# A decoder trunk reads x transposed first, applies the first norm's scale to v, q and k, and squares the MLP on ScalarE

## The chip, the cores and the metric

The kernel runs on one core of one Trainium2 chip. The metric is the time of one execution on the device in microseconds (us), lower is better. The engines: TensorE (PE in the profile; its weight loads are a row of their own, PEld), VectorE (DVE), ScalarE (ACT), GpSimd (POOL) and SyncE (SP), which issues most of the DMAs.

## The reference

Two decoder layers on 512 tokens of width 1024, all in float32. Layer 0 mixes by an attention with forget gates, layer 1 by a short gated convolution. After the mixer come an MLP with a squared ReLU and a gated per-layer embedding. Each of the three sub-layers has an RMSNorm ahead of it (of the input) or behind it (of the result).

```python
def rmsnorm(x, g):
    return x * rsqrt(mean(x * x, axis=-1) + 1e-6) * g

for i in range(2):
    hn = rmsnorm(x, g[0])
    m = fox_attention(hn, ...) if i == 0 else short_conv(hn, ...)
    x = x + rmsnorm(m, g[1])
    f = square(relu(rmsnorm(x, g[2]) @ w_up)) @ w_down        # 1024 -> 4096 -> 1024
    x = x + rmsnorm(f, g[3])
    gate = sigmoid(rmsnorm(x, g[4]) @ w_ple_gate)
    x = x + rmsnorm((p[i] @ w_ple_proj) * gate, g[5])

def fox_attention(h, w_in, b_f, w_out):                       # 16 heads of 64
    q, k, v, f = split(h @ w_in)
    c = cumsum(log_sigmoid(f + b_f))
    s = (q / 8) @ k.T + c[:, None] - c[None, :]               # causal
    return (softmax(s) @ v) @ w_out
```

The scale that the norm gives a token, r = rsqrt(mean(x * x) + 1e-6), is one number for a row of x; the gain g is one number for a column.

## The kernel before, in words

Every float32 operand of a large product is kept as two tiles, a high part rounded to the format fp32r and a low part that is the remainder. `split` (L231) makes them: ScalarE casts the high part (L233), VectorE or GpSimd subtracts (L234). `mm3` (L223) makes a product of three matmuls: high by high (L225), low stationary by high moving (L226), high stationary by low moving (L227). The names of the operands say which is which: in `v<-wh,hTl` the moving tile stands first (wh, the weight's high part) and the stationary one second (hTl, the activations' low part). Where activations are stationary (v, the mixer's output projection, the MLP's last group, the embedding's gate), the weights move; in the q/k, up and convolution projections the weights are stationary (`narrow`) and the activations move.

Weights come in tiles of 128 x 512 in a fixed order (`plan`, L97). `fetch` (L116) issues their loads on SP into 14 raw buffers, `prepare` (L136) splits them, and `wide` (L161) asks for a tile and prepares some tiles beyond it (`soon`). All other tiles share 70 pages of 128 x 512, and PSUM's eight banks are handed out by `bank`.

**The order of the instructions** on an engine is set by a scheduler with a model of the times, except inside `manual_schedule` blocks, where the engines named keep the order in which the code is written.

**The head.** `load_x` (L318) brings x in blocks of 128 tokens. For each block, `stats` (L259) lets ScalarE sum the squares (L256) and GpSimd make r (L248, L251). `scaled` (L262) multiplies x by r and g on VectorE (L264), where g was spread over the partitions by matmuls of a row with ones (L883). `turned` (L270) transposes the result on TensorE (L273), and `keep` (L276) splits it into hT. All of this for block t+1 lies between the products of block t.

**v.** `values(c, t)` (L403) makes chunk c of v for token block t: 8 products over the depth (k) into one bank. The chunks are 272 wide (the last 256 columns of v and the 16 forget-gate logits), 512 and 256. `keep_v` (L417) adds the forget bias (L419) and splits v in pieces of 64 columns (L429). `logs` (L362) and `sums_of_logs` (L384) turn the logits into running sums, with eight small matmuls (L388), which go out to DRAM and come back to each head as a bias (`bias`, L467).

**q and k.** `project(i)` (L435) makes the keys (s = 1) and queries (s = 0) of heads 2i and 2i+1, each 24 matmuls of 512 columns into one bank, and splits them from PSUM, queries with the factor 1/8 (L454, L455). The projections are woven into the loop over scores (`scores`, L485), transposes of the weights (`turn`, L509) and the mixing of v (`mix`, L523).

**The MLP** (`mlp`, L713) goes in eight groups of 512 hidden columns. `up` (L719) makes 24 matmuls for each 128 columns and applies relu on ScalarE (L731); `square` (L717) squares on VectorE. In the first seven groups the squares are taken apart into sums of quarters for a product with fewer multiplications: `halves` (L734) splits them, `quarters` (L742) makes the sums on GpSimd (L745 to L755), and `down` (L759) makes the products A11, A12, A22, S1 and so on, whose results VectorE adds up (L777). In the last group ScalarE squares straight into the high part (L807), VectorE squares again in full (L809, by L717) and subtracts for the low part, hl (L810); then `dn` uses it with activations stationary.

**The embedding's gate** weights get their gain while they are split: ScalarE multiplies by a column (L152), VectorE multiplies and subtracts in one instruction (L153).

Of the kernel before, what the change touches and what calls it, by code (L numbers as in the profile page):

```python
# [41 lines left out]
LATE = 0  # L42
PLE_OFF = 34000
# [22 lines left out]
def trunk(ctx: ExitStack, tc, g4T, x, pT, g, wv, wqk, bf, wo, wci, cw, wco, wup, wdn, wpp, wpg, out):  # L66
# [156 lines left out]
    def mm3(ps, a, b, start, stop):  # L223

        nc.tensor.matmul(ps, a.hi, b.hi, start=start, stop=False)  # L225
        nc.tensor.matmul(ps, a.lo, b.hi, start=False, stop=False)  # L226
        nc.tensor.matmul(ps, a.hi, b.lo, start=False, stop=stop)  # L227
        streamed[0] += 3 * ps.shape[-1]
        due()

    def split(hi, lo, src, eng=nc.vector):  # L231

        nc.scalar.copy(hi, src)  # L233
        eng.tensor_tensor(out=lo, in0=src, in1=hi.bitcast(F32), op=ALU.subtract)  # L234

# [82 lines left out]
    def load_x(name, t):  # L318
        xs = [page(f"{name}{t}_{n}") for n in range(2)]
        for n in range(2):  # L320
            eng = nc.scalar if name == "xa" and n else nc.sync
            eng.dma_start(xs[n][:, :S], x[t * P : (t + 1) * P, n * S : (n + 1) * S])
        return xs
# [29 lines left out]
    def attention(hT, first_x, g0, by_hand):  # L353
# [49 lines left out]
        def values(c, t, soon=SOON, between=None):  # L403

            c0, width = V_CHUNKS[c]
            n_v = min(width, D - c0)
            ps = bank(f"v{c}_{t}")
            for k in range(KT):
                if width == 256:
                    w = wide("v", c, k // 2).at(lambda u: u[:, k % 2 * 256 : k % 2 * 256 + 256])  # L410
                else:
                    w = wide("v", c, k, soon=soon)
                if k == 5 and between:
                    between()
                mm3(ps[:, :width], tokens(hT, k, t), w, k == 0, k == KT - 1)

            def keep_v():  # L417
                if n_v < width:
                    nc.vector.tensor_tensor(  # L419
                        out=logit[:, t * H : (t + 1) * H], in0=ps[:, n_v:width], in1=b_f,  # L420
                        op=ALU.add,
                    )
                for c1 in range(0, n_v, 256):
                    src = ps[:, c1 : c1 + 256].rearrange("p (i e d) -> p i e d", e=2, d=HD)
                    block = vs[t][(c0 + c1) // 256].rearrange("p (i r) -> p i r", i=2)
                    for e in range(2):
                        hi = block[:, :, 192 * e : 192 * e + HD]
                        lo = block[:, :, 64 + 64 * e : 128 + 64 * e]
                        split(hi, lo, src[:, :, e, :])  # L429

            return keep_v
# [3 lines left out]
        def project(i):  # L435
# [6 lines left out]
            for s in (1, 0):  # L442
                ps = bank(f"qk{i}_{s}")
                for k in range(KT):
# [4 lines left out]
                    if k < KT - 1:  # L449
                        yield  # L450
                if s == 0:
# [130 lines left out]
        name = "n0"  # L582
        E, done_v = mybir.EngineType, []

        def rows(t):
            r = stats(t, first_x[t], name)
            return [scaled(t, n, first_x[t], r, g0, name) for n in range(2)]

        def turn_rows(t, hs):
            for n in range(2):  # L590
                keep(t, n, turned(t, n, hs[n], name), hT)

        with tc.manual_schedule(engines={E.PE, E.DVE, E.Activation}):
            r = stats(0, first_x[0], name)
            prepare(3)
            hs = {0: [scaled(0, n, first_x[0], r, g0, name) for n in range(2)]}
            prepare(4)
            for n in range(2):
                keep(0, n, turned(0, n, hs[0][n], name), hT)
                prepare(5 + n)  # L600
            prepare(KT)
            hs[1] = rows(1)
            hs[2] = rows(2)
            for t in range(NB):
                between = (lambda: turn_rows(t + 1, hs[t + 1])) if t + 1 < NB else None
                done_v.append(values(0, t, 0, between))
                if t + 3 < NB:
                    hs[t + 3] = rows(t + 3)
                if t:
                    prepare(KT + 3 * t)  # L610
                    done_v.pop(0)()
        done_v.pop(0)()
# [9 lines left out]
        for t in range(NB):  # L622
            values(1, t)()
            if t == 2:
# [3 lines left out]
        for t in range(NB):  # L628
            values(2, t)()
# [83 lines left out]
    def mlp(l, hT, xs, then, late):  # L713
        acc = {}

        def square(out, r):
            nc.vector.tensor_tensor(out=out, in0=r, in1=r, op=ALU.mult)  # L717
# [152 lines left out]
    one = page("one")  # L870
    nc.vector.memset(one[:1, :P], 1.0)
    rows = [page(f"row{n}") for n in range(2)]
    for n in range(2):
        nc.gpsimd.dma_start(rows[n][:1, :], g[0:1, n * S : (n + 1) * S])
    with tc.manual_schedule(engines={mybir.EngineType.SP, mybir.EngineType.Activation}):
        first_x = [load_x("xa", 0)]
        fetch(4)
        first_x.append(load_x("xc", 1))
        fetch(KT)
        first_x += [load_x("xc", t) for t in (2, 3)]  # L880
    g0 = [bank(f"g0_{n}") for n in range(2)]
    for n in range(2):
        nc.tensor.matmul(g0[n], one[:1, :P], rows[n][:1, :], start=True, stop=True)  # L883
# [3 lines left out]
    lhs, opened = attention(hT, first_x, g0, by_hand)  # L887
# [106 lines left out]
```

## Time and profile before

| | |
|---|---|
| runs (three) | median 1247.38 us, 1247.27 to 1251.42 |
| the profiled execution | 1249.03 us, of which its span is 1247.3 us |
| mean granted clock of TensorE | 0.997 |
| bytes moved by DMA | 143.45 MB, mean 115 GB/s |

A row of the profile's order of time has its start and its length in us, the engine, the line, the operation, the written and read tiles and their shapes, how many instructions are merged, and in brackets how long the engine had been idle and what released it. Rows by stretch have the length, then the busy time and number of instructions (x) of each engine asked for, then the granted clock, the DMA engines' busy share and GB/s. Rows of groups have the count, the busy time, the mean length in ns, and the idle time ahead. Matmuls overlap, so that the time from one's start to the next one's start, not the length, is what one costs. In rows of waits, the numbers are us in total, times and the longest.

### The profile page before, as it was taken

The page shows a single profiled execution, that of the slowest core. Times are in us where ns is not written, and L with a number is a line of the kernel's source. Part 1 is how long each engine was busy: PE and PEld are TensorE (multiplying, and loading weights), DVE is VectorE, ACT ScalarE, POOL GpSimd, SP SyncE. Part 2 cuts the span into 40 slices and gives each one's busy share as a digit, 9 for nine tenths or more (in the row PEclk, how much of TensorE's full clock was granted, in tenths as well). Part 3 has the DMA queues.
Part 4 walks back from the last instruction along what each step waited for, and adds up shares of the span by engine and source line. Part 5 has one row for each costly group of instructions (what it writes and reads, how often), then busy time and mean ns, then how long its engine had stood idle before and what let it go on. Part 6 is the DMA issues. An engine that isn't in the chain of part 4 may idle for free.

```text
span 1247.3 us, 17921 instructions
## 1 busy us (share of the span) xinstructions
PE 1222.8 (98%) x5972; PEld 1024.7 (82%) x5972; DVE 909.4 (73%) x1386; ACT 626.1 (50%) x1325; POOL 639.4 (51%) x647
## 2 busy tenths in 40 slices
PE   7999999999999999999999999999999999999997
PEld 5888887788888888887889988889778888888785
DVE  5657787676888878979867444457778898779962
ACT  5467787555544534454655233333654345525541
POOL 2028766147878777875311000017777778778210
PEclk9999999999999999999999999999999999999999
DMA  7455442541343224427513232432422442236401
GB/s 254 150 139 157 127 123 65 160 145 56 123 135 100 77 95 135 128 68 255 142 51 106 75 96 87 162 118 69 127 62 82 136 135 93 68 110 184 137 17 52
DMA packets 82943, 143.45 MB, mean 115 GB/s; under 512 B 9825, under 2 KB 17041, under 8 KB 82849
## 3 DMA queue, kind: packets, MB, share of 16 engines
q1 hardware_dynamic: 82640, 142.03, 37.3%
q8 instruction: 47, 0.77, 0.3%
q14 instruction: 48, 0.39, 0.1%
q10 hardware_dynamic: 144, 0.26, 0.1%
q0 software_dynamic: 64, 0.00, 0.0%
HBM read 135.89 MB, written 6.37 MB: 114 GB/s over the span
## 4 chain that ended last, share of the span: by engine, by line
PE 74%; DVE 10%; POOL 5%; issue 4%; ACT 3%; DMA 3%; SPq 0%; DVEq 0%; POOLq 0%; ACTq 0%
PE dn L226 6%; PE dn L227 5%; PE up L226 5%; PE up L225 5%; PE up L227 5%; PE dn L225 5%; DVE wl L234 5%; POOL s L745 3%; PE pg L227 2%; PE pg L225 2%; PE pg L226 2%; PE qk L225 2%; PE qk L226 2%; PE qk L227 2%; DVE acc L777 2%
## 5 line engine op out<-in xcount | busy, mean ns | idle before, releaser
L234 DVE TENSOR_TENSOR wl<-raw,wh 128x512 fp32r<-128x512 f32 (+1 forms) x372 | 345.8, 979 | 27.0 <-ACT wh L233 26.7
L226 PE MATMUL up<-hTh,wl 128*128 128x512 f32 (+1 forms) x576 | 210.2, 365 | 0.0
L227 PE MATMUL up<-hTl,wh 128*128 128x512 f32 (+1 forms) x576 | 209.7, 366 | 0.0
L225 PE MATMUL up<-hTh,wh 128*128 128x512 f32 (+1 forms) x576 | 209.3, 366 | 0.0
L233 ACT CAST wh<-raw 128x512 fp32r<-128x512 f32 (+1 forms) x372 | 202.1, 619 | 1.9 <-PE ps_o L534 1.6
L234 POOL TENSOR_TENSOR wl<-T,wh 128x512 fp32r<-128x512 f32 x112 | 160.5, 1466 | 35.8 <-ACT wh L233 32.0
L225 PEld LDWEIGHTS up<-hTh,wh 128*128 128x128 f32 x576 | 108.6, 189 | 17.5
L226 PEld LDWEIGHTS up<-hTh,wl 128*128 128x128 f32 x576 | 108.6, 189 | 17.5
L227 PEld LDWEIGHTS up<-hTl,wh 128*128 128x128 f32 x576 | 108.3, 189 | 17.5
L777 DVE TENSOR_TENSOR acc<-dn,acc 128x512 f32<-128x512 f32 x168 | 107.3, 678 | 9.5 <-PE dn L227 9.4
L134 POOL TENSOR_TENSOR T<-raw,raw 128x512 f32<-128x512 f32 x56 | 88.7, 1596 | 36.9 <-DMA raw<-in_wdn 28.9
L731 ACT ACTIVATE r<-up 128x512 f32<-128x512 f32 (+1 forms) x72 | 38.7, 547 | 125.5 <-PE up L227 116.6
L134 POOL TENSOR_TENSOR T<-raw,T 128x512 f32<-128x512 f32 x56 | 91.4, 1632 | 2.2
L717 DVE TENSOR_TENSOR q<-r 128x512 f32<-128x512 f32 (+1 forms) x72 | 68.1, 952 | 29.0 <-ACT r L731 28.9
L248 POOL TENSOR_SCALAR cor_r_v<-cos,cos 128x1 f32<-128x1 f32 x4 | 1.6, 396 | 159.1 <-ACT junk L256 159.1
L233 ACT CAST A11h<-q 128x256 fp32r<-128x256 f32 x28 | 11.4, 406 | 100.7 <-DVE q L717 100.7
L233 ACT CAST wh<-T 128x512 fp32r<-128x512 f32 x112 | 61.2, 617 | 0.0
L784 POOL TENSOR_TENSOR acc<-acc,acc 128x512 f32<-128x512 f32 x28 | 46.9, 1707 | 10.0 <-DVE acc L777 10.0
L225 PE MATMUL qk<-hTh,wh 128*128 128x512 f32 x128 | 50.8, 397 | 0.0
L227 PE MATMUL qk<-hTl,wh 128*128 128x512 f32 x128 | 50.4, 394 | 0.0
L226 PE MATMUL qk<-hTh,wl 128*128 128x512 f32 x128 | 50.4, 393 | 0.0
L225 PE MATMUL pg<-wh,hTh 128*128 128x512 f32 x128 | 50.3, 393 | 0.0
(240 smaller groups left out, 3133.3 us busy)
## 6 DMA issues: line engine op xcount, KB each, us to landing
raw<-in_wup SPq DMA_DIRECT2D x128, 256.0 KB, 2.9
raw<-in_wdn SPq DMA_DIRECT2D x128, 256.0 KB, 2.8
raw<-in_wci SPq DMA_DIRECT2D x48, 256.0 KB, 3.0
raw<-in_wqk SPq DMA_DIRECT2D x32, 256.0 KB, 3.3
raw<-in_wpg SPq DMA_DIRECT2D x32, 256.0 KB, 3.6
g<-in_g SPq DMA_DIRECT2D x18, 256.0 KB, 5.7
prl<-neg_c SPq DMA_DIRECT2D x16, 256.0 KB, 6.6
raw<-in_wo SPq DMA_DIRECT2D x16, 256.0 KB, 2.8
```

Of the source, the lines that this page charges most:

```text
L134: nc.gpsimd.tensor_tensor(out=B[name, p], in0=B[a, p], in1=B[b, p], op=ALU.subtract)
L225: nc.tensor.matmul(ps, a.hi, b.hi, start=start, stop=False)
L226: nc.tensor.matmul(ps, a.lo, b.hi, start=False, stop=False)
L227: nc.tensor.matmul(ps, a.hi, b.lo, start=False, stop=stop)
L233: nc.scalar.copy(hi, src)
L234: eng.tensor_tensor(out=lo, in0=src, in1=hi.bitcast(F32), op=ALU.subtract)
L248: nc.gpsimd.tensor_scalar(out=v, in0=parts[0], scalar1=parts[1], scalar2=EPS, op0=ALU.add, op1=ALU.add)
L717: nc.vector.tensor_tensor(out=out, in0=r, in1=r, op=ALU.mult)
L731: nc.scalar.activation(r[:, :n], ps[:, :n], AF.Relu)
L745: sums = lambda out, a, b, op: nc.gpsimd.tensor_tensor(out=out, in0=a, in1=b, op=op)
L777: nc.vector.tensor_tensor(out=a, in0=banks[s], in1=a, op=ALU.add)
L784: nc.gpsimd.tensor_tensor(out=a, in0=a, in1=acc[i, s][:, :S], op=ALU.add)
```

## The change

- The host hands over x transposed as well (`xT`, eight slices of 128 columns of the model by 512 tokens) and the first gain as columns. The slices are loaded first, two of them on ScalarE's queue, each followed by the next weight tile; x itself is loaded behind them.
- `split_by` multiplies a slice by its gain while it splits it, so hT holds x times g without r. The first and second v chunks run over k in the outer loop and the four token blocks in the inner one, in four banks each (`chunk`).
- The statistics of x are taken during the second chunk. r multiplies v and the logits as they leave PSUM (`keep_v`). For q and k, four matmuls spread r over all partitions (`r_row`), and VectorE multiplies each projection by it out of PSUM, ahead of its splits, which then read a page.
- 16 matmuls of zeros (`WARM`) stand at TensorE's start; the spreading of g by matmuls, and the transposes of the first norm, go.
- The third chunk comes directly after the second, and the small matmuls of `sums_of_logs` stand after its second block.
- `square` is an activation on ScalarE.
- In `mm3` the second and third matmul change places.

```diff
     def mm3(ps, a, b, start, stop):
         nc.tensor.matmul(ps, a.hi, b.hi, start=start, stop=False)
-        nc.tensor.matmul(ps, a.lo, b.hi, start=False, stop=False)
-        nc.tensor.matmul(ps, a.hi, b.lo, start=False, stop=stop)
+        nc.tensor.matmul(ps, a.hi, b.lo, start=False, stop=False)
+        nc.tensor.matmul(ps, a.lo, b.hi, start=False, stop=stop)
...
+    def split_by(hi, lo, src, by):
+        nc.scalar.mul(hi, src, by)
+        nc.vector.scalar_tensor_tensor(
+            out=lo, in0=src, scalar=by, in1=hi.bitcast(F32), op0=ALU.mult, op1=ALU.subtract
+        )
...
+            if n_v < width:
+                nc.vector.scalar_tensor_tensor(
+                    out=logit[:, t * H : (t + 1) * H], in0=ps[:, n_v:width], scalar=r0[t],
+                    in1=b_f, op0=ALU.mult, op1=ALU.add,
+                )
+            for c1 in range(0, n_v, 256):
+                src = ps[:, c1 : c1 + 256].rearrange("p (h d) -> p h d", d=HD)
+                block = vs[t][(c0 + c1) // 256].rearrange("p (h r) -> p h r", r=P)
+                split_by(block[:, :, :HD], block[:, :, HD:], src, r0[t])
...
+                scaled_ps = page(f"qk{i}_{s}")[:, :S]
+                nc.vector.tensor_tensor(out=scaled_ps, in0=ps, in1=r_row[:, :S], op=ALU.mult)
+                ps = scaled_ps
...
+        def chunk(c, after):
+            width = V_CHUNKS[c][1]
+            banks = [bank(f"v{c}_{t}") for t in range(NB)]
+            for k in range(KT):
+                if c == 0:
+                    split_by(hT.hi[:, k, :], hT.lo[:, k, :], first_xT[k][:, :S], g0_col[:, k : k + 1])
+                w = wide("v", c, k, soon=0)
+                for t in range(NB):
+                    mm3(banks[t][:, :width], tokens(hT, k, t), w, k == 0, k == KT - 1)
+                after(k)
+            return banks
...
+            banks = {0: chunk(0, lambda k: None)}
+            def between(k):
+                t = k - 1
+                if 0 <= t < NB:
+                    r0[t] = stats(t, first_x[t], "n0")
+                    nc.gpsimd.tensor_scalar(
+                        out=every[:, (t + 1) * P : (t + 2) * P] if t < NB - 1 else diag[:, :P],
+                        in0=ident, scalar1=r0[t], scalar2=None, op0=ALU.mult,
+                    )
+                if k >= NB:
+                    keep_v(0, k - NB, banks[0][k - NB])
+                    prepare(where["v", 2, 0] + 1 + k - NB)
+            banks[1] = chunk(1, between)
+            prepare(where["qk", 0, 0] + 2)
+            spread = bank("r_row")
+            for t in range(NB):
+                nc.tensor.matmul(
+                    spread[:, t * P : (t + 1) * P], every[:, :P],
+                    every[:, (t + 1) * P : (t + 2) * P] if t < NB - 1 else diag[:, :P],
+                    start=True, stop=True,
+                )
+            for t in range(NB):
+                keep_v(1, t, banks[1][t])
+            nc.scalar.copy(r_row[:, :S], spread)
...
         for t in range(NB):
-            values(1, t)()
-            if t == 2:
+            values(2, t)
+            if t == 1:
                 sums_of_logs(tri)
...
         def square(out, r):
-            nc.vector.tensor_tensor(out=out, in0=r, in1=r, op=ALU.mult)
+            nc.scalar.activation(out, r, AF.Square)
...
     with tc.manual_schedule(engines={mybir.EngineType.SP, mybir.EngineType.Activation}):
+        nc.scalar.dma_start(g0_col, g0T)
+        for k in range(KT):
+            (nc.scalar if k < 2 else nc.sync).dma_start(first_xT[k][:, :S], xT[k])
+            fetch(k + 1)
+        first_x = []
+        for t in range(NB):
+            fetch(KT + t + 1)
+            first_x.append(load_x("xc", t))
+    idle = bank("idle")
+    for _ in range(WARM):
+        nc.tensor.matmul(idle[:, :P], warm[:, :P], warm[:, :P], start=True, stop=True)
```

More of the change, by code (lines that the diff above doesn't have):

```diff
@@ L42 @@
 LATE = 0
+WARM = 16
 PLE_OFF = 34000
@@ L867, in ple @@
                 then(t)
[L870 to L874, printed above, removed]
-    with tc.manual_schedule(engines={mybir.EngineType.SP, mybir.EngineType.Activation}):
[L876 to L883, printed above, removed]
+    g0_col = consts.tile([P, KT], F32, tag="g0_col", name="g0_col")
+    warm = page("warm")
+    nc.vector.memset(warm[:, :S], 0.0)
+    first_xT = [page(f"xT{k}") for k in range(KT)]
+    with tc.manual_schedule(engines={mybir.EngineType.SP, mybir.EngineType.Activation}):
+        nc.scalar.dma_start(g0_col, g0T)
[9 more added lines that the diff above has]
+        nc.tensor.matmul(idle[:, :P], warm[:, :P], warm[:, :P], start=True, stop=True)
     kept = dram.tile([2, NB, 2, P, S], F32, tag="kept", name="kept")
```

71 lines of the change are left out of this document (16 added, 55 removed).

## The prediction

> **What bounds the kernel now.** I read the page's busy times first, then the order of time over the first 66 us, then the waits, then tables by stretch.
>
> ```profile
> PE 1222.8 (98%) x5972; PEld 1024.7 (82%) x5972; DVE 909.4 (73%) x1386; ACT 626.1 (50%) x1325; POOL 639.4 (51%) x647
> ```
>
> PE is the bound: a change pays only where PE stands still, runs at a low rate or does work that can go. Each matmul also has a weight load of its own (5972 and 5972), though the scores issue two running with the same stationary tile: a stationary operand that stays saves nothing here. The head, in order of time:
>
> ```profile
> 0.79 0.41 ACTq L322 DMA_DIRECT2D xa<-in_x  x1
> ...
> 6.35 3.75 PE L883 MATMUL g<-row,one 1*128 1x512 f32 x4 [6.35 <-DMA row<-in_g]
> ...
> 10.02 2.02 PE L273 MATMUL n_p<-ident,n_h 128*128 128x128 f32 x8
> ...
> 11.81 0.59 PE L225 MATMUL v<-wh,hTh 128*128 128x272 f32 x1
> ...
> 13.16 0.43 PE L225 MATMUL v<-wh,hTh 128*128 128x272 f32 x1
> ...
> 13.38 0.43 PE L226 MATMUL v<-wh,hTl 128*128 128x272 f32 x1
> ...
> 18.29 0.29 PE L227 MATMUL v<-wl,hTh 128*128 128x272 f32 x1
> ...
> 18.41 0.29 PE L225 MATMUL v<-wh,hTh 128*128 128x272 f32 x1
> ...
> 21.19 0.53 POOL L615 MEMSET ones<- 128x512 f32 x1
> ...
> 28.11 0.40 PE L227 MATMUL v<-wl,hTh 128*128 128x512 f32 x1
> ...
> 28.34 0.39 PE L225 MATMUL v<-wh,hTh 128*128 128x512 f32 x1
> ```
>
> ```profile
> 64.86 0.28 PE L226 MATMUL v<-wh,hTl 128*128 128x256 f32 x1
> 64.98 0.28 PE L227 MATMUL v<-wl,hTh 128*128 128x256 f32 x1
> 65.10 0.40 PE L225 MATMUL qk<-hTh,wh 128*128 128x512 f32 x1
> ```
>
> ```profile
> 47.05 1.17 PE ps_c L388 x8
> ```
>
> Durations of overlapping matmuls mislead; start-to-start counts. A 272-wide one takes 0.22 us early (13.16 to 13.38) and 0.125 us later (18.29 to 18.41), a 512-wide one 0.23, a 256-wide one 0.12. The first useful product starts at 11.81, behind the norm (DMA, squares, broadcast of g, scaling, transposes), and the v stage ends at 65.10. Its own matmuls need 96 x 0.126 + 96 x 0.227 + 96 x 0.12 + 1.17 (ps_c) = 12.1 + 21.8 + 11.5 + 1.2 = 46.6 us. So 18.5 us of this head are start, transposes, waits and the low early rate.
>
> **The head.** Gone from PE: the broadcast of g and 32 transposes; from the path: statistics and scaling ahead of the first product. Gains multiply the transposed x while it is split, and r goes on v, q and k afterwards.
>
> ```profile
> raw<-in_wv SPq DMA_DIRECT2D x8, 136.0 KB, 3.9
> ...
> xa<-in_x ACTq DMA_DIRECT2D x1, 256.0 KB, 4.1
> ```
>
> ```profile
> L153 DVE SCALAR_TENSOR_TENSOR wl<-raw,g,wh 128x512 fp32r<-128x512 f32 x32 | 22.6, 744 | 0.0
> ...
> L152 ACT ACTIVATE wh<-raw,g 128x512 fp32r<-128x512 f32 x32 | 21.2, 712 | 1.5 <-ACT wh L152 1.4
> ```
>
> ```profile
> L234 DVE TENSOR_TENSOR wl<-raw,wh 128x272 fp32r<-128x272 f32 x8 | 3.1, 434 | 6.5 <-ACT wh L233 6.5
> ...
> L233 ACT CAST wh<-raw 128x272 fp32r<-128x272 f32 x8 | 2.8, 416 | 0.0
> ```
>
> ```profile
> 10.00:20.00 10.00, 8.35 (x44) 6.99 (x44) 7.61 (x14) 7.56 (x19) 1.73 (x4) 1.00 1.00 361
> ```
>
> ScalarE's queue issues the gain column at 0.79 and x's first slice at 1.2; with 4.1 us to landing it is there at 5.3. Then high half 0.71 and weight cast 0.42 on ScalarE: first product possible at 6.4. VectorE's low halves (0.74 + 0.43 after the high half) let the second go at 7.2. After that each k needs 401 KB, 1.11 us at the 361 GB/s of 10 to 20 us (DMA share 1.00); 1.13 us of ScalarE, 1.18 us of VectorE; and 12 x 0.126 = 1.5 us of PE. PE paces it.
>
> The 16 warm products are plain fp32. Two such calls on g made four records in 3.75 us, 0.94 us for 512 columns; at 128 columns 32 records x 0.23 = 7.5 us at that rate, half at the full one. They start after a memset like L615's 0.53, at about 1.5, and end between 5.3 and 9.0. That is also the bound of their harm: they can hold the first product to 9.0 at most. Between data at 7.2 and 9.0 I take 7.8.
>
> The early low rate bears on that. The Trainium skill, page "TensorE: Matmul & The Clock Gate", Part 1, says that TensorE runs at half clock until about 3.4 us of sustained work have filled a free-running window. By it the warm products would open the clock between 4.9 and 8.3 (an estimate: 1.5 and one to two windows) and chunk 0 would start at the full rate. The trace agrees on the factor (0.22 against 0.125) but not on the delay: work began at 6.35 and the low rate still held at 13.4. If the warm products (zeros, fp32) don't count, the first useful ones run low for some 3 us, as from 11.81 on: 14 products at 0.1 us each, 1.4 us, inside the range.
>
> From 7.8: 12.1 + 21.8 + 0.9 (r's spread: eight records of 0.115) + 11.5 + 1.2 = 55.3, against 65.1: 9.8 us. The hand-overs cost something. ps_c now stands after the second of four last-chunk tiles, about 48.4, while forget-gate logs can start on ScalarE and VectorE only when chunk 1's v is kept, about 43, and need some 4 to 5 us. I take 0.8 us (bounds 0 and 5). **Head: -9.0** (from 9.8 - 1.2 - 5 = 3.6 with warm products until 9.0 and the full wait, to 9.8 + 0.6 = 10.4 with data at 7.2 and none). Statistics, x's second read and POOL's diagonals lie beside chunk 1's 21.8 us. x is read once more, 2 MB, 5.8 us of DMA. SP queues it behind what chunk 0 needs (3.2 MB, in by about 14) and among chunk 1's first four weights (in by about 23, while chunk 1 starts at 19.9 and takes one per 2.7 us). On ScalarE and VectorE the keeping of v waits for a chunk's end with weight casts queued behind it; those run a k or more ahead of PE.
>
> **The scaling of q and k.** Each of 16 projection halves gets a VectorE product of PSUM with r's row ahead of its splits. The row is copied by ScalarE at about 44; the first half ends near 61, so nothing queues behind that.
>
> ```profile
> L861 DVE TENSOR_TENSOR e<-pp,gate 128x512 f32<-128x512 f32 x16 | 11.0, 688 | 27.7 <-PE pp L227 17.6 <-ACT gate L858 10.0
> ```
>
> ```profile
> 72.00:180.00 108.00, 108.00 (x563) 92.02 (x562) 80.32 (x230) 82.62 (x198) 69.71 (x117) 1.00 0.49 133
> 180.00:200.00 20.00, 18.22 (x97) 14.70 (x96) 17.26 (x49) 17.55 (x44) 14.05 (x23) 0.98 0.47 119
> 558.00:590.00 32.00, 30.81 (x136) 25.22 (x135) 31.55 (x35) 15.19 (x26) 20.01 (x12) 1.00 0.78 247
> ```
>
> ```profile
> 90.57 0.69 DVE L455 SCALAR_TENSOR_TENSOR q<-qk,q 64x512 fp32r<-64x512 f32 x1
> ```
>
> ```profile
> 94.98 0.28 PE L493 MATMUL sc<-kh,q 128*128 128x256 f32 x1
> ```
>
> The same shape costs 0.69 us (L861), so 11 us of VectorE. Up to 180 us VectorE is busy 80 of 108 and PE stands nowhere; pair 1's last q split ends at 91.26, its first scores run at 94.98: 3.7 us of slack against 0.69. Free there, unless that slack goes. Between 180 and 200 VectorE (17.3 of 20) and ScalarE (17.6) are nearly full and PE already loses 1.8 us; the last pair's two products fall there, 1.4 us, and I let 1.2 through. The projection's bank comes free sooner, after one product instead of six splits, which speaks for less, down to all 1.8 won. **+1.2** (-1.8 to +4).
>
> ```profile
> 200.00:220.00 20.00, 19.85 (x106) 0.94 0.11 27
> ```
>
> Behind those stops the granted clock is 0.94 over 20 us, 1.2 us lost, which goes or stays with them.
>
> **The squares.**
>
> ```profile
> L717 DVE TENSOR_TENSOR q<-r 128x512 f32<-128x512 f32 x56 | 56.3, 1005 | 25.3 <-ACT r L731 25.2
> ```
>
> ```profile
> 581.32 0.63 ACT L807 ACTIVATE hh<-r 128x512 fp32r<-128x512 f32 x1
> ```
>
> ```profile
> 583.64 0.68 DVE L717 TENSOR_TENSOR q<-r 128x512 f32<-128x512 f32 x1
> ```
>
> ```profile
> 293.99 0.62 ACT L233 CAST A12h<-q 128x512 fp32r<-128x512 f32 x1 [2.30 <-DVE q L717]
> ```
>
> ```profile
> PE dn L226 <- DVE hl L810: 2.5, 2, 1.3
> ```
>
> ```profile
> 294.00:305.60 11.60, 11.07 (x43) 1.00 0.01 2
> ...
> 354.00:560.00 206.00, 206.00 (x910) 1.00 0.36 108
> ...
> 870.80:882.40 11.60, 11.07 (x43) 1.00 0.00 0
> ```
>
> A 128x512 square is 1.005 us on VectorE, 0.63 on ScalarE (L807). The Trainium skill speaks against the move: "ScalarE: Activation LUTs", Rules for kernel authors, wants relu and products on VectorE, up to three times as fast in bf16. The rows of this fp32 kernel say the reverse.
>
> What it is worth is only where PE waits in the MLP. In steady groups (910 matmuls in 206 us, 0.226 each) that is nothing. In a layer's last group PE waits for hl, 2.5 us in all; ahead of that hl VectorE has a square at 583.64, in a stretch where it is busy 31.55 of 32. Without three squares, 0.68 or more each, hl is ready 2 us sooner: **-2.5**. At the first group PE makes 43 matmuls in 11.6 us, 11.6 - 43 x 0.226 = 1.9 us lost per layer, 3.7 in both, and ScalarE waits there 2.3 us for a square queued on VectorE. With both on ScalarE that crossing goes; then POOL's sums for S1 are next late. I take **-3.0** (0 to -3.7). Scheduling outside the hand-ordered blocks is done afresh, so the order may differ. ScalarE gains some 45 us, at 50% busy.
>
> **The order in each product.** Each bank gets the same three matmuls: time moves only at a wait. With activations stationary their low part has one product, 0.23 us, more; in up, q/k and conv products weights are stationary, so there the words don't hold: the weights' low part goes third. I take 0, bounds 1 us either way.
>
> **Sum**, against the profiled execution's 1249.03 us (span 1247.3): -9.0 + 1.2 - 2.5 - 3.0 = -13.3, 1235.7. The median of the runs is 1247.38, 1.65 us lower, so I forecast 1234.
>
> **Rivals.** (a) The squares bring nothing: PE's wait goes over to POOL's sums or to ScalarE's queue, which must then pass casts, relu and square in order. For it: POOL's part of that chain is untouched. Against: 31.55 of 32. 1247.4 - 9.0 + 1.2 = 1239.6. (b) The head gives 3.6, its lower bound, instead of 9.0. For it: the low rate at 13.4, the forget-gate chain. 1239.5; with (a), 1245. (c) Slower: VectorE becomes the pace of attention. Were its 14 extra products from 72 us on all waited for, 9.7 us, and its 28 half-wide splits, which now read SBUF, stretched as L717 is (1.005 against 0.68; +0.33 each, 9.2 us), then 1247.4 - 14.5 + 18.9 = 1251.8. It decides once each added product costs PE over 1.0 us (14.5 us over 14). For it: 86% busy at 180 to 200. Against: 3.7 us of slack and 28 idle us before 180.
>
> **How the numbers follow.** Forecast 0.62 (1228 to 1238); (a) 0.18; (b) 0.10; (a) and (b) together 0.07; (c) 0.03. All gains at their bounds give 1247.4 - 10.4 - 6.2 - 1.8 - 1.2 - 1 = 1226.8; the range, 1227 to 1242, leaves out (a) with (b), (c) and tails of (a) and (b) above. Half a per cent, 6.2 us, is about what a measurement of this kernel tells from no change: below 1241.2 is faster. Faster 0.88 (the forecast and (a), (b) nearly whole), same 0.09, slower 0.03.
>
> **What would show it.** First v product near 8 instead of 11.8, at 0.125 us from the start; first q/k product near 56; no wait of dn for hl; 294 to 305's count near 226 ns a matmul; PE without new gaps from 65 to 180. Wrong: scores waiting for q or k; ps_c or the second v chunk waiting for ScalarE; dn waiting for S1 as long as before.

## The result, and the profile after

The changed kernel takes 1231.31 us (median of four runs, 1230.88 to 1231.62), the kernel before beside it 1247.65 us: a ratio of 0.9862, 95% interval 0.9843 to 0.9881. The profiled execution went from 1249.03 to 1231.44 us, 17.6 us less. The clock times at which certain matmuls start tell in which stage (us from the span's start):

| mark | before | after | change of the stage that ends there |
|---|---|---|---|
| first product of v | 11.81 | 8.01 | -3.80 |
| first product of q and k | 65.10 | 56.24 | -5.06 (head in all: -8.86) |
| last product of the attention's output projection | 265.21 | 256.57 | +0.22 |
| first product of the convolution (MLP 0 lies before it) | 663.55 | 650.64 | -4.27 |
| first up-product of MLP 1 | 843.12 | 830.20 | -0.01 |
| end | 1247.32 | 1229.69 | -4.71 |

So half comes from the head, half from the two MLPs, and attention gives nothing back. The line of busy time on the page after:

```profile
PE 1213.8 (99%) x5976; PEld 1025.7 (83%) x5976; DVE 857.4 (70%) x1306; ACT 673.5 (55%) x1382; POOL 642.2 (52%) x650
```

VectorE gave up 52 us and ScalarE took 47; TensorE, the bound, shed only 9 of busy time, the rest was standing still. The head in order of time, changed kernel:

```profile
1.22 0.93 ACTq L892 DMA_DIRECT2D xT<-in_xT  x2
1.50 5.90 PE L900 MATMUL idle<-warm 128*128 128x128 f32 x32 [1.50 <-DVE warm L887]
...
5.63 1.28 ACT L239 ACT_TABLE_LOAD   x1 [5.63 <-DMA xT<-in_xT]
...
6.93 0.72 ACT L239 ACTIVATE hTh<-xT,g_col 128x512 fp32r<-128x512 f32 x1
7.55 0.40 ACT L234 CAST wh<-raw 128x272 fp32r<-128x272 f32 x1
...
8.01 0.39 PE L226 MATMUL v<-wh,hTh 128*128 128x272 f32 x1 [0.61 <-ACT wh L234]
...
8.84 0.39 PE L227 MATMUL v<-wl,hTh 128*128 128x272 f32 x1 [0.44 <-DVE wl L235]
...
11.82 0.29 PE L226 MATMUL v<-wh,hTh 128*128 128x272 f32 x1
11.95 0.28 PE L227 MATMUL v<-wl,hTh 128*128 128x272 f32 x1
...
56.24 0.40 PE L226 MATMUL qk<-hTh,wh 128*128 128x512 f32 x1
```

The first product waits for the weight's cast, and that stands behind the slice's high half on ScalarE. Ahead of both is a row that the prediction does not have: ScalarE loads its function table for 1.28 us, and begins only when x's slice has landed, because the load stands with the first activation. From the first product on the clock is open: 11.82 to 11.95 is 0.125 us, where the kernel before paid 0.22 at the same time of day.

The MLP, groups of instructions by line, and TensorE's part of two stretches that start 2.4 us behind the first product of `down`, as those of the prediction did:

```profile
L732 ACT ACTIVATE q<-r 128x512 f32<-128x512 f32 x56 | 35.3, 630 | 2.1
```

```profile
285.80:297.40 11.60, 11.60 (x53) 1.00 0.01 2
858.00:869.60 11.60, 11.60 (x53) 1.00 0.01 1
```

A square is 0.63 us on ScalarE, and TensorE has no gap left: 53 products where 43 stood, 11.60 busy of 11.60. In the list of waits of the changed kernel, no product of `down` waits for anything any more; these are the longest rows of TensorE that are left behind the head:

```profile
PE n_p L281 <- DVE n_h L272: 1.3, 2, 0.9
PE ps_o L536 <- ACT ph L234: 1.2, 2, 0.7
```

### The profile page after: what moved, and what is told of

Read it like the earlier page. It is cut to its first block, busy times and chain, and to the rows that moved or that the text cites. A ratio compares the mean times of both kernels' runs of the same rounds, so it can differ in the third digit from the quotient of the medians.

```text
span 1229.7 us, 17957 instructions
## 1 busy us (share of the span) xinstructions
PE 1213.8 (99%) x5976; PEld 1025.7 (83%) x5976; DVE 857.4 (70%) x1306; ACT 673.5 (55%) x1382; POOL 642.2 (52%) x650
## 4 chain that ended last, share of the span: by engine, by line
PE 91%; DVE 3%; ACT 2%; DMA 2%; issue 1%; POOL 1%; SPq 0%; DVEq 0%; POOLq 0%; ACTq 0%
PE up L228 9%; PE up L226 9%; PE up L227 9%; PE dn L228 8%; PE dn L227 8%; PE dn L226 8%; PE pg L228 2%; PE pg L226 2%; PE pg L227 2%; PE qk L226 2%; PE qk L227 2%; PE qk L228 2%; PE v L227 1%; PE sc L495 1%; PE v L228 1%; PE v L226 1%
## 5 line engine op out<-in xcount | busy, mean ns | idle before, releaser
L235 DVE TENSOR_TENSOR wl<-raw,wh 128x512 fp32r<-128x512 f32 (+1 forms) x372 | 352.3, 993 | 24.6 <-ACT wh L234 16.7
L235 POOL TENSOR_TENSOR wl<-T,wh 128x512 fp32r<-128x512 f32 x112 | 155.9, 1421 | 32.6 <-ACT wh L234 31.3
L235 DVE TENSOR_TENSOR A12l<-q,A12h 128x512 fp32r<-128x512 f32 x28 | 24.5, 876 | 50.9 <-ACT A12h L234 50.9
L235 DVE TENSOR_TENSOR A11l<-q,A11h 128x256 fp32r<-128x256 f32 x28 | 25.4, 906 | 40.6 <-ACT A11h L234 40.6
```

## The experiments

**The MLP: squares and order, each alone and each undone.** Theory: TensorE's waits in the first and the last group go because the squares leave VectorE; the order in the products moves nothing. Rival: the order carries part of it, or the gain comes from elsewhere.

Squares on ScalarE, alone, on the kernel before:

```diff
-            nc.vector.tensor_tensor(out=out, in0=r, in1=r, op=ALU.mult)
+            nc.scalar.activation(out, r, AF.Square)
```

> The kernel before with the squares on ScalarE and nothing else. Theory: the whole 9.0 us that the MLPs gained comes from the squares alone, so about 1238.6 against 1247.6; no wait of dn for hl, and from 294 to 306 us each matmul near 226 ns. Rival 1: part of it comes from the new order in each product (0.23 us more for each low part at the three kinds of waits), then 1241 or more. Rival 2: it comes from another schedule in the changed kernel as a whole, then this edit alone gives between 0 and 5 us.

Measured: 1242.12 us against 1249.14 before (0.9944, 0.9929 to 0.996): 7.0 us less instead of the theory's 9.0, so the rest hangs on something else. Order of the second and third matmul, alone, on the kernel before:

```diff
-        nc.tensor.matmul(ps, a.lo, b.hi, start=False, stop=False)
-        nc.tensor.matmul(ps, a.hi, b.lo, start=False, stop=stop)
+        nc.tensor.matmul(ps, a.hi, b.lo, start=False, stop=False)
+        nc.tensor.matmul(ps, a.lo, b.hi, start=False, stop=stop)
```

> The kernel before with the second and third matmul of each product changed places and nothing else. Theory: no change, 1247.6 within 1 us, since a bank gets the same matmuls and few waits stand between the second and the third. Rival 1: the low part's 0.23 us at every wait takes 2 us or more off, 1245.6 or less.

Measured: 1251.01 us, slower by 0.2% (1.0019, 1.0009 to 1.0028). The changed kernel with the squares back on VectorE:

```diff
-            nc.scalar.activation(out, r, AF.Square)
+            nc.vector.tensor_tensor(out=out, in0=r, in1=r, op=ALU.mult)
```

> The changed kernel with the squares back on VectorE. Theory: it loses the 9.0 us of the MLPs and keeps head and attention, about 1240.3, with the waits for hl and for A12 and S1 back. Rival 1 (the order in each product): a part of the waits stays away, 1237 or less. Rival 2 (schedule): anything between 1231 and 1240, without the waits coming back at the same places.

Measured: 1242.03 us (0.9951, 0.9937 to 0.9966), 10.7 above the changed kernel. The changed kernel with the old order:

```diff
-        nc.tensor.matmul(ps, a.hi, b.lo, start=False, stop=False)
-        nc.tensor.matmul(ps, a.lo, b.hi, start=False, stop=stop)
+        nc.tensor.matmul(ps, a.lo, b.hi, start=False, stop=False)
+        nc.tensor.matmul(ps, a.hi, b.lo, start=False, stop=stop)
```

> The changed kernel with the old order in each product. Theory: 1231.3 within 1 us; at the head the second product then waits for the activations' low part (7.68 to 8.43 us) instead of the weight's (8.78), which could bring 0.4 us forward. Rival 1: 2 us slower or more.

Measured: 1233.4 us (0.9878, 0.9861 to 0.9894), 2.1 above the changed kernel.

The four traces together show where. For each matmul of `down`, take the time from its start to the next start, less the usual one (0.227 us for 512 columns), and add up what is over by more than 0.02 us. By place in the layer, us lost in layer 0 and layer 1:

| | first group | second group | groups between | last group | first to last `down` product |
|---|---|---|---|---|---|
| before | 2.16, 2.15 | 0.77, 0.84 | 0, 0 | 1.55, 1.70 | 312.7, 312.9 |
| squares alone | 0, 0 | 1.88, 1.88 | 0, 0 | 0.09, 0.09 | 310.0, 310.0 |
| order alone | 2.29, 2.25 | 0, 0 | 0.11, 0.60 | 2.73, 4.25 | 313.3, 315.4 |
| both (the changed kernel) | 0, 0 | 0, 0 | 0, 0 | 0.09, 0.09 | 308.1, 308.1 |
| changed, old order | 0, 0 | 1.83, 0.88 | 0, 0 | 0.09, 0.09 | 310.0, 309.0 |
| changed, squares on VectorE | 2.33, 2.32 | 0, 0 | 0, 0.71 | 1.93, 4.97 | 312.4, 316.2 |

The squares clear the first and the last group, whatever the order. The second group is cleared by the order, whatever the squares: with squares alone TensorE there waits for the low half of A12, in order of time:

```profile
339.22 1.07 PE L225 MATMUL dn<-wh,A12h 128*128 128x512 f32 x4
341.24 0.50 PE L226 MATMUL dn<-wh,A12l 128*128 128x512 f32 x1 [0.94 <-DVE A12l L234]
```

Four products with the high half run, then the product that needs the low half is next in turn. With the low half third, the product with the weight's low half goes between, and A12l is there in time. The same order without the moved squares is worse than the old one: the last group then has hl later (2.3 to 2.4 us of wait where before had 1.2 to 1.3), and in layer 1 the clock falls behind the wait:

```profile
1159.56 0.39 PE L225 MATMUL dn<-wh,hh 128*128 128x512 f32 x1
1162.23 0.50 PE L227 MATMUL dn<-wh,hl 128*128 128x512 f32 x1 [2.29 <-DVE hl L810]
...
1163.10 0.63 PE L225 MATMUL dn<-wh,hh 128*128 128x512 f32 x1
1163.53 0.63 PE L226 MATMUL dn<-wl,hh 128*128 128x512 f32 x1
```

The products from 1163.10 on start 0.43 us apart instead of 0.227. That hl comes later is VectorE's doing: in layer 1 TensorE comes to the place as early as before (its last up-product starts 288.6 us behind the layer's first `down` product in both), but VectorE, which has no idle time there, starts this hl at 293.9 us instead of 293.0. The order of VectorE's instructions differs between the two kernels up to 273 us; what moved its queue back is not shown. The prediction's "order: 0" holds for neither case.

Where the squares pay was asked once more by leaving them on VectorE in groups 2 to 6 of the changed kernel:

```diff
-        def square(out, r):
-            nc.scalar.activation(out, r, AF.Square)
+        def square(out, r, gr=7):
+            if gr in (0, 1, 7):
+                nc.scalar.activation(out, r, AF.Square)
+            else:
+                nc.vector.tensor_tensor(out=out, in0=r, in1=r, op=ALU.mult)
...
-                square(q[f][:, lo:hi], r[:, : hi - lo])
+                square(q[f][:, lo:hi], r[:, : hi - lo], gr)
```

> The changed kernel with the squares on ScalarE only in the groups 0, 1 and 7 of each MLP, on VectorE in the groups 2 to 6. Theory: a square pays only where PE waits, and it waited in the first two groups and the last, so 1231.3 within 1 us. Rival: VectorE's load as such matters (68 us of squares, 43 of them in the groups 2 to 6), then a good part of the 9 us comes back, 1234 or more.

Measured: 1232.84 us (0.9876, 0.9861 to 0.9891), 1.5 more than the changed kernel. 40 of the 56 wide squares are back on VectorE, and cost 0.53 us of gaps in layer 0 and 1.25 in layer 1, against 10.7 for all of them. What counts is the three groups where TensorE waited, not the 41 us of VectorE time that the 40 squares take.

**The head: warm products, table, first loads.** Theory: the early low rate is ended by the 16 warm products; without them the first useful products run low.

```diff
-WARM = 16
+WARM = 0
```

> The changed kernel without the 16 products of zeros. Theory: the first v products run at half rate until a free-running window of sustained work is over, at 0.1 us more for each 272-wide product: 3 to 7 us of low rate, 1.4 to 3.4 us lost, 1232.7 to 1234.7. Rival: the products of zeros do nothing for the clock and it opens by itself, then 1231.3 and the same intervals from the first product on.

Measured: 1234.06 us (0.9882, 0.9865 to 0.9898); the first q/k product at 57.77 instead of 56.24. In order of time, without warm products:

```profile
7.41 0.59 PE L226 MATMUL v<-wh,hTh 128*128 128x272 f32 x1 [7.41 <-ACT wh L234]
...
8.63 0.43 PE L228 MATMUL v<-wh,hTl 128*128 128x272 f32 x1
8.86 0.43 PE L226 MATMUL v<-wh,hTh 128*128 128x272 f32 x1
```

Nineteen products start 0.227 us apart, until 12.9, at 0.10 more than 0.125: 1.9 us lost, against 0.6 won by starting at 7.41; the first q/k product comes 1.53 us later than in the changed kernel. So zeros in fp32 do open the clock. In the changed kernel the warm records start 0.213 us apart until 5.9 and 0.111 from there, 4.4 us after the first. The Trainium skill, page "TensorE: Matmul & The Clock Gate", Part 1, has the half rate last until about 3.4 us of sustained work fill a free-running window. The 4.4 us and the 5.5 from 7.41 to 12.9 lie between one such window and two. Over all kernels with 16 warm products it took from 3.1 us (three products by r's row) to 6.0 us (table early), so the shortest was a little less than one window.

Then the table load, pulled ahead by a one-column square of the zeros between the DMA issues for slices 0 and 1:

```diff
+    early = stat("early")
...
+            if k == 1:
+                nc.scalar.activation(early, warm[:, :1], AF.Square)
```

> The changed kernel with one tiny activation on the zeros ahead of the first slice's arrival, so that ScalarE's table load (1.28 us, which began only at 5.63 when the first slice had landed) is over before it. Theory: the load lies on the path of the first product, so 1.3 us less, 1230.0, with the first v product near 6.7. Rival: the first product then waits for something else that is as late (weights, gain column, the products of zeros until 7.4), and nothing changes.

Measured: 1230.13 us (0.985, 0.9835 to 0.9865). In order of time:

```profile
1.50 6.67 PE L903 MATMUL idle<-warm 128*128 128x128 f32 x32 [1.50 <-DVE warm L887]
2.19 1.28 ACT L896 ACT_TABLE_LOAD   x1 [2.19 <-issue]
...
4.97 0.72 ACT L239 ACTIVATE hTh<-xT,g_col 128x512 fp32r<-128x512 f32 x1 [1.28 <-DMA xT<-in_xT]
5.60 0.40 ACT L234 CAST wh<-raw 128x272 fp32r<-128x272 f32 x1
7.50 0.72 ACT L239 ACTIVATE hTh<-xT,g_col 128x512 fp32r<-128x512 f32 x1 [1.50 <-DMA xT<-in_xT]
7.93 0.37 PE L226 MATMUL v<-wh,hTh 128*128 128x272 f32 x1
```

Operands are ready at 6.0, but the first product still starts at 7.93: the warm products hold TensorE until then (they ran at the low rate until 7.4 in this execution). The first q/k product comes 0.8 us sooner than in the changed kernel, as the second product follows the first at once. But other kernels with the same head as the changed kernel put it anywhere from 55.33 us (squares back on VectorE, where x's first slice landed at 4.64 us) to 56.24 (the changed kernel, 5.56), and this kernel's 55.43 lies among them; the intervals of the two times overlap too. That the early table alone won anything is not shown. And x's second slice landed only at 7.5. Hence the last version: fewer warm products, slices first on their queue, the gain on SP, the weight's split ahead of the slice's.

```diff
-WARM = 16
+WARM = 8
...
+                w = wide("v", c, k, soon=0)
                 if c == 0:
                     split_by(hT.hi[:, k, :], hT.lo[:, k, :], first_xT[k][:, :S], g0_col[:, k : k + 1])
-                w = wide("v", c, k, soon=0)
...
-        nc.scalar.dma_start(g0_col, g0T)
+        nc.sync.dma_start(g0_col, g0T)
...
+            if k == 1:
+                nc.scalar.activation(early, warm[:, :1], AF.Square)
```

> The changed kernel with its head pulled together: a tiny square on zeros ahead of x's first slice brings ScalarE's table in early, x's slices 0 and 1 are the first two on ScalarE's queue, the gain column goes first on SP, chunk 0 splits the weight before the slice, and 8 warm products instead of 16. Theory (the first product stood behind the table load of 1.28 us, and then behind the warm products): slice 0 lands near 3.1, the weight near 4.4 to 5.6, the first product comes at 5 to 6 instead of 8.01. But slice 1 and the next weights land at 5 to 7, and the clock opens only between 5.5 and 8, so of the 2 to 3 us about half comes through: 1 to 2 us below the changed kernel, 1229.3 to 1230.3, and the first q/k product at 54.5 to 55.5 instead of 56.24. Rival (the head is bound by the arrival of data behind the first product, or by the clock): the first product comes sooner but the first q/k product stays within 0.5 of 56.2, and the time within 0.5 us of 1231.3.

Measured: 1228.7 us (1227.75 to 1230.11; 0.9832, 0.9816 to 0.9849), the lowest time of all kernels here, though its interval overlaps the changed kernel's. The first product of v comes at 5.93, the first q/k product at 54.00: 2.24 us sooner than in the changed kernel, and 1.33 sooner than in any kernel with the changed kernel's head. Four things were altered at once, so it is not shown which of them counts. In the profiled execution 1.3 us is left at the end; it was the slowest of the four (1230.11, the others 1227.75 to 1228.88). In order of time, behind the scores of the last pair:

```profile
187.52 0.35 PE L537 MATMUL ps_o<-pl,v 128*128 128x256 f32 x1 [0.35 <-DVE pl L235]
188.62 0.50 PE L536 MATMUL ps_o<-ph,v 128*128 128x512 f32 x1 [0.74 <-ACT ph L234]
188.96 0.58 PE L495 MATMUL sc<-kh,q 128*128 128x512 f32 x1
189.34 0.63 PE L495 MATMUL sc<-kl,q 128*128 128x512 f32 x1
```

and by stretch:

```profile
185.58:188.99 3.41, 2.29 (x12) 1.47 (x12) 3.35 (x10) 2.99 (x7) 3.41 (x9) 1.00 0.43 117
188.99:192.40 3.41, 3.41 (x10) 2.64 (x9) 3.29 (x11) 2.84 (x8) 2.67 (x6) 0.50 0.00 0
```

Eight products from 188.96 on start 0.38 to 0.43 us apart, with a granted clock of 0.50 (behind GpSimd's column). The changed kernel has the same two waits, 0.35 and 0.74 us, and does not pay this:

```profile
190.12 0.35 PE L537 MATMUL ps_o<-pl,v 128*128 128x256 f32 x1 [0.35 <-DVE pl L235]
191.22 0.51 PE L536 MATMUL ps_o<-ph,v 128*128 128x512 f32 x1 [0.74 <-ACT ph L234]
191.56 0.40 PE L495 MATMUL sc<-kh,q 128*128 128x512 f32 x1
191.80 0.40 PE L495 MATMUL sc<-kl,q 128*128 128x512 f32 x1
```

```profile
186.77:190.18 3.41, 3.04 (x18) 2.21 (x18) 3.31 (x13) 2.67 (x9) 2.77 (x8) 1.00 0.69 191
190.18:193.59 3.41, 2.67 (x11) 1.93 (x12) 3.31 (x8) 3.18 (x8) 2.68 (x4) 1.00 0.21 59
```

The traces' records of the granted clock tell why. From the time when it opens (4.67 us in the last version, 5.86 in the changed kernel) it changes only after whole multiples of 3.413 us, and the fall at 188.99 lasts one such step. Count TensorE's work in a step as 0.2265 us for 512 columns (an estimate from the start-to-start times). In the last version both waits stand in the step ahead of the fall, which holds 1.01 us of work; in the changed kernel they stand in two steps, with 1.73 and 2.21. Over the 13 traces with such a record the clock falls 21 times, always behind a step with 1.13 us of work or less, and no step at the full clock without a fall behind it has less than 1.10. So the same wait costs a slow stretch or not by where it lies on that grid, which is counted from the opening of the clock and so differs from one execution to the next.

**Attention: the product by r's row.** Theory: slack takes it up. Rival: it costs its share, and something else hides it. First without it (this kernel leaves r out of q and k):

```diff
-                scaled_ps = page(f"qk{i}_{s}")[:, :S]
-                nc.vector.tensor_tensor(out=scaled_ps, in0=ps, in1=r_row[:, :S], op=ALU.mult)
-                ps = scaled_ps
```

> The changed kernel without the product of q and k by r's row: r is left out of q and k, the splits read PSUM again. Theory (one product is taken up by slack): no difference above 1 us, 1230.3 to 1232.3, attention 200 +-0.7 us. Rival (the single product costs its share too, and what the changed kernel wins elsewhere in attention hides it): 3 to 10 us less, 1221 to 1228. Third reading: if the sooner release of the bank was worth something, it comes out slower, by up to 1.8 us.

Measured: 1229.53 us (1228.68 to 1230.92; 0.9843, 0.9828 to 0.9858). From the first q/k product to the last output product it takes 200.29 us, the changed kernel 200.33. But the parts differ. Without the product, in order of time:

```profile
189.21 0.50 PE L533 MATMUL ps_o<-ph,v 128*128 128x512 f32 x1 [1.19 <-ACT ph L234]
...
190.53 0.63 PE L492 MATMUL sc<-kl,q 128*128 128x512 f32 x1
190.95 0.63 PE L226 MATMUL o<-wh,hTh 128*128 128x512 f32 x1
```

Between 72 and 206 us, adding up as for the MLP (the usual time is taken by shape), it loses 8.0 us in waits and 1.5 in a slow stretch; the changed kernel loses 9.6, all in waits, as its clock does not fall. So the product costs 1.6 us of waits, and a slow stretch that did not occur in that execution hides it. By the medians of the runs this kernel is 1.8 us faster, though the intervals overlap. The kernel before had the slow stretch as well (1.7 us). The waits lie in one place, in the mixing of the first heads. By stretch, TensorE first, in the changed kernel and without the product:

```profile
104.00:114.00 10.00, 9.09 (x48) 7.10 (x46) 7.59 (x24) 7.37 (x19) 7.75 (x12) 1.00 0.49 138
```

```profile
104.00:114.00 10.00, 10.00 (x56) 8.67 (x55) 7.20 (x24) 8.09 (x22) 6.39 (x13) 1.00 0.55 124
```

Counted from each kernel's first q/k product, the stretch from 44.6 to 66.9 us loses 1.8 to 2.6 us in the seven traces with one product by r's row, and 0.9 in the four without it (before, squares alone, order alone, this one). At the last pairs, from 111.5 to 156.1 us, both kinds lose 6.1 to 6.8 us in waits.

Then more of the same work. Two and three products instead of one, written to the same page:

```diff
-                nc.vector.tensor_tensor(out=scaled_ps, in0=ps, in1=r_row[:, :S], op=ALU.mult)
+                for _ in range(3):
+                    nc.vector.tensor_tensor(out=scaled_ps, in0=ps, in1=r_row[:, :S], op=ALU.mult)
```

> The changed kernel with the multiplication of each projection half by r's row done three times over, 22 us more of VectorE in the attention. Theory: the slack of 2.6 to 7.8 us ahead of the scores hides 1.4 us more each; only where VectorE is nearly full, at the end of the projections, some comes through: 0 to 3 us, 1231.3 to 1234.3. Rival (VectorE close to setting the pace): most of the 22 us comes through, 1242 or more.

Measured: 1252.38 us (1.0029, 1.0017 to 1.0041), slower than the kernel before. With `range(2)`:

> Two products of each projection by r's row instead of one (the same page written twice): 16 more products of 0.69 us, 11 us of VectorE. Theory (VectorE's queue is at its limit in attention, so each product beyond the first comes through whole): half of what three products cost, attention +9 to +11 us, 1240 to 1242. Rival (what slack there is takes a second one too, and only the third overflows): +0 to +3 us, 1231 to 1234.

Measured: 1239.92 to 1240.78 us in three executions (0.9927, 0.9911 to 0.9944). The profiled one took 2482.65 us with every matmul at half its usual rate from first to last, so its trace is not read here. And three products' work, of which two hang on nothing:

```diff
+                spare = page(f"spare{i}_{s}")[:, :S]
+                for _ in range(2):
+                    nc.vector.tensor_tensor(out=spare, in0=r_row[:, :S], in1=r_row[:, :S], op=ALU.mult)
```

> The same VectorE work as with three products by r's row, but two of them multiply r's row by itself into a page that nobody reads: 22 us of VectorE that hang on nothing, in the same place of its code. Theory (what costs is VectorE's time, in order, whatever it hangs on): about as slow as three products in the chain, attention +15 to +22 us, 1246 to 1253. Rival (what costs is the chain from a projection's last matmul through the products to q and k): the load beside it goes into the gaps, +0 to +4 us, 1231 to 1235.

Measured: 1241.65 us (0.9938, 0.9924 to 0.9953), between the theory and its rival. Taken against the changed kernel, 16 more products in the chain (10.9 us of VectorE) cost 9 us, 32 cost 21, and 32 beside it cost 10 (medians). Rows by stretch, 72 to 190 us: length, then busy time and count of TensorE, its weight loads, VectorE, ScalarE, GpSimd. First the changed kernel:

```profile
72.00:190.00 118.00, 116.42 (x612) 98.02 (x610) 98.67 (x277) 94.21 (x224) 81.95 (x135) 1.00 0.49 139
```

three products in the chain:

```profile
72.00:190.00 118.00, 109.39 (x542) 88.23 (x541) 100.76 (x266) 82.17 (x196) 73.51 (x122) 1.00 0.46 121
```

two of them beside it:

```profile
72.00:190.00 118.00, 112.58 (x584) 94.42 (x583) 107.76 (x282) 89.00 (x209) 85.62 (x126) 1.00 0.49 131
```

VectorE is busier in the case that loses less. So it is not its load alone: work in the chain from a projection to q and k costs nearly its whole length, work beside it about half. TensorE stops in the mixing of v both times, but behind different engines. With three products in the chain, ScalarE waits for the last one, casts k, and the high part of the weights of v (ph) stands behind that in its queue:

```profile
199.77 1.26 ACT L234 CAST kh<-qk 64x512 fp32r<-64x512 f32 x2 [2.70 <-DVE qk L452]
...
202.20 0.95 ACT L234 CAST ph<-pT 128x512 fp32r<-128x512 f32 x2
202.83 0.79 PE L537 MATMUL ps_o<-ph,v 128*128 128x512 f32 x1 [3.68 <-ACT ph L234]
```

Seven stops of this kind come to 10.1 us. With two of them beside it, the low part (pl) stands in VectorE's queue behind a spare product and k's low half:

```profile
190.12 0.68 DVE L454 TENSOR_TENSOR spare<-r_row 128x512 f32<-128x512 f32 x1
190.72 1.40 DVE L235 TENSOR_TENSOR kl<-qk,kh 64x512 fp32r<-64x512 f32 x2
192.15 0.69 DVE L235 TENSOR_TENSOR pl<-pT,ph 128x512 fp32r<-128x512 f32 x1
...
192.90 0.50 PE L540 MATMUL ps_o<-pl,v 128*128 128x512 f32 x1 [1.42 <-DVE pl L235]
```

Six stops of this kind come to 4.2 us.

## Why the prediction was right, and where its sizes were off

The forecast was 1234.0 us, 13.3 below; the time is 1231.3, inside the range. Against the profiled executions the sum said 1235.7 and 1231.44 came, 4.3 us less. By its terms:

- **The head, -9.0: measured -8.86.** The first product at 8.01 instead of 7.8, the stage from it to q and k 48.2 us where 12.1 + 21.8 + 0.9 + 11.5 + 1.2 + 0.8 = 48.3 was worked out. That both came out so close is in part luck. The 7.8 was a middle between operands ready at 7.2 and warm products until 9.0; in truth the slice landed at 5.56 (5.3 was reckoned), the warm products ended at 7.40, and the table load of 1.28 us, which is no term of the sum, stood between the slice and its first use. Kernels with the same head had their first product anywhere from 7.20 to 8.01. And the 0.8 us put down for the hand-overs was not lost at ps_c, which waited for nothing, but in the first chunk (0.7 us), whose second product came 0.83 us behind the first. Rival (b), the head at 3.6, falls.
- **The scaling, +1.2: measured +0.22** for all of attention. The size of the term was near, 1.6 us of waits between the kernels with and without the product, but its place was wrong, so that is luck: the last pair's products cost nothing, and the waits came at 104 to 114 us, where the prediction had "Free there, unless that slack goes". What it left standing, "1.2 us lost, which goes or stays with them", went: the slow stretch did not occur in this execution (1.7 us before), by where the stops lay on the grid of the clock, which no term of the sum covers.
- **Rival (c)** needed each added product to cost over 1.0 us. One product costs 1.6 / 16 = 0.10, and even the next 32 cost 20.4 / 32 = 0.64 each in attention. Its mechanism is there, though, one product further on: the second already comes through at four fifths of its length. 3.7 us of slack in front of the scores was the wrong place to look; the stops of the experiments come at the mixing of v.
- **The squares, -5.5, and the order, 0: measured -9.0 together.** This is the mis-sized term. First group 4.3 us instead of 3.0, though its working had 3.7 in reach. Even that was short by the edges: a stretch counts the products that overlap its ends, 53 without a gap where 11.6 / 0.2265 = 51 fit, so that of the 43 about 41.5 were whole, and 11.6 - 41.5 x 0.2265 = 2.2 us a layer was lost instead of 1.9. Last group 3.1 instead of 2.5, since the wait that the profile lists (1.2, 1.3) leaves out the start-up behind it (1.55, 1.70 by starts). Second group 1.6 instead of 0: "in steady groups that is nothing" was read from 354 us on, and the second group's gaps lie at 342 to 346. Sum 9.0. Rival (a), the squares bring nothing, falls with the kernel that has them undone: 1242.03.
- **The step that failed** is "the order in each product: I take 0, bounds 1 us either way". It is worth 1.9 and 0.9 us in the two layers with the squares moved, by the second group's wait for a low half, and costs 0.6 and 2.6 without. "Time moves only at a wait" was the right rule; the waits for low halves in the second group were not looked up (A12l stands among the waits of before with 0.5 us in all):

```profile
PE dn L226 <- DVE A12l L234: 0.5, 2, 0.3
```


Left open: what moves VectorE's queue back with the order alone; what the early table and each of the other edits of the last version are worth by themselves; and whether its head keeps its 2.24 us if the waits at 188 us are taken away. That was not tried, though its three other executions, 2.4 to 3.6 us below the changed kernel's median, speak for it.

## What to carry to other kernels

Price a move off an engine by the groups in which the bound engine waits, the second group after a start included, and by start-to-start times instead of the listed waits: here 40 of 56 moved squares were worth 1.5 us, and the others the rest of 10.7. An order inside a product and the engine of its operands are one decision, since the order alone cost time and paid only with the squares moved. At the start, two things are worth trying, shown here only together: a tiny activation ahead of the first one that waits for a load, and a warm-up that ends when the data is due.

## What the runs showed of the hardware that was not expected

- Stops of TensorE far shorter than the opening time of the clock can throw it back to the half rate, for one step of 3.41 us. Behind idle times of 1.06 (kernel before, at 198.31), 1.19 (without the scaling, 189.21) and 0.74 us (last version, 188.62), some eight products of 512 columns started 0.4 us apart; behind 0.74 us in the changed kernel (191.22) and 1.20 with the order alone (198.22) none did. What tells them apart is the work in the step: 1.13 us or less of 3.41 in all 21 falls. The same page and part of the Trainium skill has the clock close after an idle window of about 3.4 us. Here steps that were at work for up to a third of their time closed it, so on this the measurement decides; the page's free-running window is what the records show.
- The table load (1.28 us) waits for the data of the activation behind it, as at 5.63; the same load at 2.19, ahead of a one-column activation on zeros, runs while ScalarE is idle.
- The head's low rate does not show in the granted clock: the first 10 us read 1.00 in the changed kernel, while the warm products ran at half rate. The record of the clock begins with its opening (5.86 us), and the column reads 1.00 where there is no record: in the execution of 2482.65 us there is none at all. Start-to-start times show the low rate; the column showed the later stretches (0.50 from 188.99 us in the last version).
